# Output weights' squares taken a group ahead in quarters, and their split in halves, in a hybrid attention layer

## The chip, the cores and the metric

One Trainium2 chip, one of its cores. The metric is the device time of one execution in microseconds (us): the median of 3 runs is 599.39 (599.29 to 605.95). The engines are named as in the profile: PE (TensorE matmul), PEld (its weight load), DVE (VectorE), ACT (ScalarE), POOL (GpSimd), SP (SyncE, which issues most DMAs here).

## The reference

One encoder layer over 1024 tokens of width 1024, in float32. The input is normalised, one projection makes the columns of two head groups, both are gated, and a second projection `w_out` of 1024 x 1024 is added to the residual and normalised:

```python
h = _rmsnorm(x, norm_gain[l])
proj = h @ w_in[l]
q_a, k_a, v_a, g_a, q_b, k_b, v_b, g_b = jnp.split(proj, split_at, axis=-1)
...
o_a = _gqa_blocked(q_a, k_a, v_a) * jax.nn.silu(g_a)
o_b = _neighbourhood_attn(q_b, k_b, v_b, na_rpb[l])   # 8 heads, over a 16 x 64 grid
o_b = o_b * jax.nn.silu(g_b)
mixed = jnp.concatenate([o_a, o_b], axis=-1)
x = x + mixed @ w_out[l]
...
return _rmsnorm(x, final_norm_gain)
```

## The kernel before

**Numbers in two parts.** Matmuls run in float16. Each float32 operand is scaled and split into a high part and a residual (low part), and a product is three matmuls: high x high, high x low, low x high. So a group of weights has to be prepared before PE can use it.

**Groups of weights.** The weights come in 17 groups of 256 columns: 0 to 12 of `w_in`, 13 to 16 of `w_out`. A group is `raw[g]`, 128 partitions x 8 x 256 in float32 (1 MB). Its preparation has five steps. `load_w` issues its load on POOL's queue; `raw` has two buffers, so group g + 2 is loaded when group g is split. `prep_a` squares it on ACT and adds up each partition (`wss`). `prep_b` sums over the partitions by a one-column matmul on PE into the PSUM tile that the next projection will use, and DVE and POOL make the scale of it. `prep_c` writes the high part as two copies on ACT (`whl`), and `prep_d` the residual as two instructions on DVE.

**Steps.** The program is laid out in steps of a class `Flow`. In the stage of this document (from about 355 us on) a step takes one head of one block of 128 tokens of the neighbourhood attention: 8 blocks x 8 heads. "Head 4_3" below is head 3 of block 4, and the order prints its maximum as `mx4_3`. A step computes the head's scores on PE (`b_qk`, L674 and L675), the biased scores and their maximum on DVE (L682, L684), and two exponentials on ACT (L685, L686); in the next step the residual of the exponentials on DVE and its transposing DMA on SP (`b_lo`, L691, L693); and five steps on, the product with the values on PE (`b_pv`, L704 to L706). Between scores and products each step fills PE with about three chunks of 6 projection matmuls (`fill`; L368 in the profile): the gates of groups 9 to 12, then the output projection `out_gen`, which takes blocks 0 to 3 through group 13, then 14, 15 and 16, and block 4 behind them. DVE adds its result to the residual rows `x2b` (L773), which are loaded on POOL's queue (L764). `at(delay, position, ...)` puts a piece of work so many steps later.

**What sets the order.** PE's instructions stay as they are written. Behind the opening block, those of ACT, DVE, POOL and SP are put in order by a scheduler when the program is built, by its own idea of what will be ready; each engine then runs its list in order. So a piece can stand several steps ahead of where `at` put it.

**Where the preparation starts.** `prep(g + 1)` is called when the first chunk of group g starts. It puts `prep_a` one or two steps later (`PREP`), and `pend`, one step on, lets `sums_now` call `prep_b` in the middle of the next projection; `prep_c` and `prep_d` follow a step later, then the load of g + 2.

Of the kernel before, what the change touches and what calls it, by code (L numbers as in the profile page):

```python
# [10 lines left out]
BF16 = mybir.dt.bfloat16  # L11
# [5 lines left out]
P = 128  # L17
KC = 8
# [14 lines left out]
LN_P = 14.0 * float(np.log(2.0))  # L33
# [10 lines left out]
class Flow:  # L44
# [8 lines left out]
    def at(self, delay, pos, fn, *a):  # L53
        self.due.setdefault((self.slot + delay, pos), []).append((fn, a))
# [35 lines left out]
def kernel(ctx: ExitStack, tc: tile.TileContext, x: bass.AP, w: bass.AP, wo: bass.AP,  # L90
# [57 lines left out]
    def tn(name, n=1, tag="t"):  # L148
        return tiny.tile([P, n], F32, tag=tag, name=name)
# [47 lines left out]
    def col(i, n=1):  # L197
        return sm[:, i:i + n]
# [68 lines left out]

    wss = {}

    def prep_a(g):  # L270
        if g < 15:
            t = whl.tile([P, 2, KC, GC], F16, tag="whl", name=f"whl{g}")
        else:
            if g == 15:
                late["w"] = one.tile([P, 2, 2, KC, GC], F16, tag="hT0", name="whl15")
            t = late["w"][:, g - 15]
        wp[g] = (t[:, 0], t[:, 1])
        wss[g] = tn(f"wss{g}", 1, "ws")
        if g:
            act.activation(wp[g][0].bitcast(BF16), raw[g], AF.Square, accum_out=wss[g])  # L280
            return
        late["half"] = tn("wssh", 1, "ws")
        act.activation(wp[g][0][:, :4].bitcast(BF16), raw[g][:, :4], AF.Square, accum_out=late["half"])

    def prep_a2(g):
        dve.tensor_tensor_reduce(out=wp[g][0][:, 4:].bitcast(BF16), in0=raw[g][:, 4:], in1=raw[g][:, 4:], scale=1.0,
                                 scalar=late["half"], op0=OP.mult, op1=OP.add, accum_out=wss[g])

    def prep_b(g):
        pt = ahead.append(proj_tile(f"wt{g}")) or ahead[-1]  # L290
        top = [a.bitcast(BF16)[:, 1:2] for a in (mh[:, :1], wss[g])]
        pe.matmul(pt[:, 0, :1], top[0].to_broadcast([P, P]), top[1], start=True, stop=True)
        dve.tensor_scalar(wss[g], pt[:, 0, :1], -2.0 ** -27, 1e-30, op0=OP.mult, op1=OP.add)  # L293
        pool.tensor_tensor(col(S_ + g), wss[g], mh[:, :1], op=OP.pow)  # L294

    def prep_c(g):
        for i in range(0, KC, KC // 2):
            s = slice(i, i + KC // 2)
            act.activation(wp[g][0][:, s], raw[g][:, s], AF.Copy, scale=col(S_ + g))  # L299

    def prep_d(g):
        ready.add(g)
        n = KC if g == 0 else KC // 2
        for i in range(0, KC, n):
            s = slice(i, i + n)
            dve.scalar_tensor_tensor(wp[g][1][:, s], raw[g][:, s], col(S_ + g), wp[g][0][:, s], op0=OP.mult, op1=OP.subtract)  # L306
# [8 lines left out]
    ready = set()  # L315

    def prep_e(g):
        dve.reciprocal(col(RC + g), col(S_ + g))
# [725 lines left out]
```

## Time and profile before

| | |
|---|---|
| median of the runs | 599.39 us |
| the profiled execution | 600.28 us, span 598.5 us |
| mean granted PE clock | 0.974 |
| busy, share of the span | PE 89%, DVE 74%, ACT 65%, POOL 20% |
| whole squares of groups 13 to 16 on ACT start at | 457.06, 474.88, 481.91, 502.17 us |
| their first copies on ACT start at | 471.64, 489.26, 507.89, 525.18 us |
| their loads are issued by POOL at | 397.40, 426.95, 475.58, 496.08 us |

A row of a timeline gives start, duration, engine, line, operation, what is written and read, the size and the count; in brackets stands how long the engine sat idle ahead of it, and what released it. `wt` and `po` are PSUM tiles of projections, `whl` the two parts of weights, `mhl` those of the mixed rows. The times of a count of several run from the first start to the last end.

### The profile page before, as it was taken

Reading aid. Unit: us, or ns where it says so; the run is one execution under the profiler, and the core shown is the slowest. Engines: PE = TensorE matmul, PEld = TensorE weight load, DVE = VectorE, ACT = ScalarE, POOL = GpSimd, SP = SyncE. Lnnn points to the kernel's source line nnn. Section 1 sums busy time; section 2 is a strip of 40 time slices with the busy share of each in tenths; the row PEclk is TensorE's granted clock in tenths of the full one; section 3 lists DMA queues with packets and bytes.
Section 4 is the critical chain, followed back from the end, with each engine's and each line's share of the span. In section 5 each row is a group of like instructions: output and inputs, shape, how many; then the busy total and the mean of one; then the engine's idle time right before and its main releaser. Section 6 shows DMA issues by size and latency. Waiting matters only on the chain.

```text
span 598.5 us, 13870 instructions
## 1 busy us (share of the span) xinstructions
PE 530.8 (89%) x5541; PEld 404.4 (68%) x5541; DVE 440.9 (74%) x986; ACT 391.0 (65%) x647; POOL 121.8 (20%) x150
## 2 busy tenths in 40 slices
PE   2587989979979989998989979999999789889894
PEld 1366878758856545556768857887877567668684
DVE  4689676987978968975988947585878767778332
ACT  5553445777768858875868826677779986774210
POOL 2395788510100000000100000010111221122100
PEclk9979989989999989999899999999999899999898
DMA  8989533799999999999899983467576996699422
GB/s 233 225 162 243 112 108 68 143 187 215 195 192 188 206 209 181 221 191 208 179 188 213 230 214 79 90 133 96 128 116 123 180 200 146 138 146 190 92 61 70
DMA packets 245972, 97.26 MB, mean 162 GB/s; under 512 B 236562, under 2 KB 237202, under 8 KB 243987
## 3 DMA queue, kind: packets, MB, share of 16 engines
q1 hardware_dynamic: 242306, 75.66, 70.8%
q0 software_dynamic: 3312, 19.92, 11.7%
q8 instruction: 43, 0.70, 0.5%
q10 hardware_dynamic: 288, 0.79, 0.5%
q14 instruction: 23, 0.18, 0.1%
HBM read 31.33 MB, written 4.19 MB: 59 GB/s over the span
## 4 chain that ended last, share of the span: by engine, by line
PE 48%; DMA 18%; DVE 14%; issue 8%; ACT 5%; POOL 4%; SPq 1%; DVEq 0%; POOLq 0%; ACTq 0%
PE pj L368 15%; DMA ar<-ar 10%; PE wt L368 8%; PE kb L368 5%; PE po L368 4%; PE s L591 3%; PE s L593 3%; PE pv L622 2%; PE pv L624 2%; PE pv L623 2%; DVE whl L306 2%; DMA ar<-mhl 2%; POOL nt L416 1%; PE sb L675 1%; DMA x2b<-in_x_dram 1%
## 5 line engine op out<-in xcount | busy, mean ns | idle before, releaser
L368 PEld LDWEIGHTS <-hT 128*128 128x128 f16 x2112 | 205.8, 100 | 68.9 <-DMA hT<-xhl 14.7
L368 PE MATMUL pj<-whl,hT 128*128 128x256 f16 x1584 | 187.6, 274 | 3.9 <-DMA hT<-xhl 2.5
L602 ACT ACTIVATE ar<-s,nm,sm 128x1024 f32<-128x1024 f32 x64 | 76.9, 1202 | 43.6 <-DVE nm L600 35.8
L600 DVE CUSTOM_DVE_ANT_0 ar<-s,sm 128x1024 bf16<-128x1024 f32 x64 | 81.9, 1279 | 18.9 <-PE s L593 18.6
L368 PE MATMUL wt<-whl,hT 128*128 128x256 f16 x528 | 70.9, 294 | 13.8 <-ACT whl L299 7.1
L608 DVE TENSOR_TENSOR ar<-ar 128x1024 f16<-128x1024 f32 x64 | 77.9, 1218 | 5.4 <-ACT ar L603 5.4
L603 ACT ACTIVATE ar<-ar 128x1024 f16<-128x1024 f32 x64 | 67.5, 1056 | 6.5 <-DVE ar L608 5.3
L368 PE MATMUL po<-whl,mA 128*128 128x256 f16 x384 | 65.8, 277 | 0.0
L685 ACT ACTIVATE rq<-ar,mx,sm 128x384 f32<-128x384 f32 (+1 forms) x64 | 43.0, 672 | 30.8 <-DVE mx L684 30.6
L294 POOL TENSOR_TENSOR sm<-wss,mh 128x1 f32<-128x1 f32 x17 | 12.7, 749 | 240.4 <-DVE wss L293 160.6
L368 PEld LDWEIGHTS <-mA 128*128 128x128 f16 x512 | 48.8, 100 | 12.5 <-issue 5.3
L368 PE MATMUL po<-whl,ar 128*128 128x256 f16 x192 | 53.1, 277 | 0.0
L622 PE MATMUL pv<-va,ar 128*128 128x64 f16 x384 | 39.9, 195 | 12.0 <-DMA ar<-ar 12.0
L306 DVE SCALAR_TENSOR_TENSOR whl<-raw,sm,whl 128x1024 f16<-128x1024 f32 (+1 forms) x33 | 44.7, 1371 | 2.3 <-ACT whl L299 2.3
L622 PEld LDWEIGHTS <-ar 128*128 128x128 f16 x384 | 35.1, 99 | 16.6 <-DMA ar<-ar 14.3
L686 ACT ACTIVATE ar<-ar,mx,sm 128x384 f16<-128x384 f32 (+1 forms) x64 | 42.8, 673 | 1.0
L299 ACT ACTIVATE whl<-raw,sm 128x1024 f16<-128x1024 f32 x34 | 37.0, 1136 | 5.9 <-POOL sm L294 5.8
L624 PE MATMUL pv<-va,ar 128*128 128x64 f16 x384 | 39.9, 195 | 0.0
L623 PE MATMUL pv<-va,ar 128*128 128x64 f16 x384 | 39.8, 195 | 0.0
L591 PE MATMUL s<-kTa,rq 128*128 128x512 f16 x128 | 39.4, 391 | 0.3 <-ACT ar L602 0.3
L682 DVE CUSTOM_DVE_ANT_0 ar<-sb,bias 128x384 f32<-128x384 f32 x48 | 26.6, 554 | 17.2 <-PE sb L675 14.3
L691 DVE TENSOR_TENSOR ar<-rq,ar 128x384 f16<-128x384 f32 (+1 forms) x64 | 34.1, 533 | 4.4 <-ACT ar L686 4.4
(183 smaller groups left out, 1012.2 us busy)
## 6 DMA issues: line engine op xcount, KB each, us to landing
raw<-in_w_dram POOLq DMA_DIRECT2D x11, 1024.0 KB, 6.3
raw<-in_wo_dram POOLq DMA_DIRECT2D x4, 1024.0 KB, 6.1
ar<-in_x_dram SPq DMA_DIRECT2D x7, 512.0 KB, 6.4
khh<-ar SPq DMA_DIRECT2D x16, 128.0 KB, 4.1
x2b<-in_x_dram POOLq DMA_DIRECT2D x4, 512.0 KB, 6.4
x<-in_x_dram POOLq DMA_DIRECT2D x4, 512.0 KB, 6.3
out_dram<-x2b SPq DMA_DIRECT2D x8, 256.0 KB, 3.3
ar<-ar SPq DMA_TRANSPOSE x112, 4.5
```

Source lines behind the costliest of these rows:

```text
L306: dve.scalar_tensor_tensor(wp[g][1][:, s], raw[g][:, s], col(S_ + g), wp[g][0][:, s], op0=OP.mult, op1=OP.subtract)
L368: pe.matmul(*o[0], **o[1])
L591: pe.matmul(s[:, c * 512:(c + 1) * 512], q, kTa[:, 4 * c:4 * c + 4, hh], start=True, stop=False)
L600: dve.tensor_tensor_reduce(out=hl[:, 1].bitcast(BF16), in0=s, in1=col(SHA).to_broadcast([P, 1024]), scale=col(NSA), scalar=3e38, op0=OP.ad ...
L602: act.activation(p32, s, AF.Exp, bias=nm, scale=col(SCA), accum_out=sums[hh, u][:, h:h + 1])
L603: at(0, "post", lambda: act.activation(hl[:, 0], p32, AF.Copy))
L608: dve.tensor_tensor(hl[:, 1], p32, hl[:, 0], op=OP.subtract)
L622: pe.matmul(o, pt[:, kt], va[:, kt, hh, 0], start=kt == 0, stop=False)
L623: pe.matmul(o, pt[:, kt], va[:, kt, hh, 1], start=False, stop=False)
L624: pe.matmul(o, pt[:, 8 + kt], va[:, kt, hh, 0], start=False, stop=kt == 7)
L685: act.activation(p32, t, AF.Exp, bias=mx, scale=col(SCB + hh), accum_out=sums["b", u][:, h:h + 1])
L686: act.activation(hl[:, 0], t, AF.Exp, bias=mx, scale=col(SCB + hh))
```

## The change

For groups 13 to 16 the squares are taken in quarters (`prep_q`, four ACT instructions of 128x512 with one `wss` column each, whose unused output goes to a free place in `rq`) and one group earlier: those of 13 in steps 7 to 10 behind the start of group 11, those of g + 1 in steps 2 and 3 behind the start of group g - 1's projection. `prep_b` then adds four one-column matmuls instead of one. `prep_c` and `prep_d` run in halves, in steps 1 and 2 after `prep(g)`, and the load of g + 2 follows in step 3. Groups 0 to 12 stay as they were, but for the order around them.

```diff
+SQ13 = (7, 8, 9, 10)
...
-PREP = {2: 4, 3: 0, 4: 2, 12: 0, 13: 0}
+PREP = {2: 4, 3: 0, 4: 2, 12: 0}
...
-    def prep_a(g):
+    def alloc_wp(g):
...
         wp[g] = (t[:, 0], t[:, 1])
-        wss[g] = tn(f"wss{g}", 1, "ws")
+
+    def prep_a(g):
+        alloc_wp(g)
+        wss[g] = [tn(f"wss{g}", 1, "ws")]
...
+    def prep_q(g, i):
+
+        junk = carve(rq, 17408, [512], BF16).rearrange("p (k c) -> p k c", c=GC)
+        if i == 0:
+            wss[g] = [tn(f"wss{g}_{k}", 1, "ws") for k in range(4)]
+        act.activation(junk, raw[g][:, 2 * i:2 * i + 2], AF.Square, accum_out=wss[g][i])
...
     def prep_b(g):
         pt = ahead.append(proj_tile(f"wt{g}")) or ahead[-1]
-        top = [a.bitcast(BF16)[:, 1:2] for a in (mh[:, :1], wss[g])]
-        pe.matmul(pt[:, 0, :1], top[0].to_broadcast([P, P]), top[1], start=True, stop=True)
-        dve.tensor_scalar(wss[g], pt[:, 0, :1], -2.0 ** -27, 1e-30, op0=OP.mult, op1=OP.add)
-        pool.tensor_tensor(col(S_ + g), wss[g], mh[:, :1], op=OP.pow)
-
-    def prep_c(g):
-        for i in range(0, KC, KC // 2):
-            s = slice(i, i + KC // 2)
+        top = [a.bitcast(BF16)[:, 1:2] for a in (mh[:, :1], *wss[g])]
+        n = len(wss[g])
+        for i in range(n):
+            pe.matmul(pt[:, 0, :1], top[0].to_broadcast([P, P]), top[1 + i], start=i == 0, stop=i == n - 1)
+        t = wss[g][0]
+        dve.tensor_scalar(t, pt[:, 0, :1], -2.0 ** -27, 1e-30, op0=OP.mult, op1=OP.add)
+        pool.tensor_tensor(col(S_ + g), t, mh[:, :1], op=OP.pow)
+        scaled.add(g)
+
+    HALVES = [slice(i, i + KC // 2) for i in range(0, KC, KC // 2)]
+
+    def prep_c(g, halves=HALVES):
+        assert g in scaled
+        for s in halves:
             act.activation(wp[g][0][:, s], raw[g][:, s], AF.Copy, scale=col(S_ + g))
 
-    def prep_d(g):
+    def prep_d(g, halves=HALVES):
+        for s in halves if g else [slice(0, KC)]:
+            dve.scalar_tensor_tensor(wp[g][1][:, s], raw[g][:, s], col(S_ + g), wp[g][0][:, s], op0=OP.mult, op1=OP.subtract)
+        if halves[-1] != HALVES[-1]:
+            return
         ready.add(g)
...
+    def squares(g, slots):
+        for i, k in enumerate(slots):
+            at(k, "pre", prep_q, g, i)
+        at(slots[-1], "mid", pend.append, g)
+
     def prep(g):
-        d = PREP.get(g, 1)
-        at(d + 1, "pre", prep_a, g)
-        at(d + 2, "mid", pend.append, g)
+        if g < 13:
+            d = PREP.get(g, 1)
+            at(d + 1, "pre", prep_a, g)
+            at(d + 2, "mid", pend.append, g)
+            if g == 12:
+                squares(13, SQ13)
+            return
+        at(1, "pre", alloc_wp, g)
+        for i, h in enumerate(HALVES):
+            at(1 + i, "pre", prep_c, g, [h])
+            at(1 + i, "post", prep_d, g, [h])
+        if g + 2 < 17:
+            at(3, "pre", load_w, g + 2)
+        if g < 16:
+            squares(g + 1, (2, 2, 3, 3))
 
     def sums_now():
...
             prep_b(g)
+            if g > 12:
+                continue
             at(1, "pre", prep_c, g)
             at(1, "post", prep_d, g)
```

Line numbers grow by 36 from `prep` on: the scores are L710 and L711 after the change, maxima L718 and L720, exponentials L721 and L722, transposes L729, products L740 to L742, the projection L404, sums L809; quarters are L294, copies L316, residuals L320.

What the build's scheduler made of it, at three places. First ACT around head 4_3, where group 13's squares stood. Before:

```order
L686 ACTIVATE ar_78<-ar_78,mx4_2_5961,sm_97 128x384
L561 ACTIVATE ar_78<-pj11_3_5929,sm_97 128x512
L280 ACTIVATE whl13_6089,wss13_6090<-raw13_5183 128x2048
L685 ACTIVATE rq_79,sumb4_5856<-ar_78,mx4_3_6001,sm_97 128x384
L685 ACTIVATE rq_79,sumb4_5856<-ar_78,mx4_4_6050,sm_97 128x384
```

and of the change:

```order
L721 ACTIVATE rq_79,sumb4_5871<-ar_78,mx4_2_5975,sm_97 128x384
L597 ACTIVATE ar_78<-wt13_5853,sm_97 128x512
L316 ACTIVATE whl13_6103<-raw13_5183,sm_97 128x1024 x2
L721 ACTIVATE rq_79,sumb4_5871<-ar_78,mx4_3_6015,sm_97 128x384
L722 ACTIVATE ar_78<-ar_78,mx4_2_5975,sm_97 128x384
L722 ACTIVATE ar_78<-ar_78,mx4_3_6015,sm_97 128x384
L768 ACTIVATE mhl3_6119,os3_6118<-mA1_1063 128x512
```

The squares (L280, `wss13`) have become the copies (L316) at the same place, and the second exponentials of heads 4_2 and 4_3 stand behind them. Both halves stand together.

Second, ACT from head 4_6 to 5_1, ahead of the start of group 13's projection on PE. Before:

```order
L685 ACTIVATE rq_79,sumb4_5856<-ar_78,mx4_7_6179,sm_97 128x384
L686 ACTIVATE ar_78<-ar_78,mx4_7_6179,sm_97 128x384
L732 ACTIVATE mhl4_6443,os4_6442<-mA2_1064 128x512
L685 ACTIVATE rq_79,sumb5_6218<-ar_78,mx5_0_6219,sm_97 128x384
L732 ACTIVATE mhl5_7136,os5_7135<-mA2_1064 128x512
L299 ACTIVATE whl13_6089<-raw13_5183,sm_97 128x1024 x2
L686 ACTIVATE ar_78<-ar_78,mx5_0_6219,sm_97 128x384
L561 ACTIVATE ar_78<-pj12_3_6188,sm_97 128x512
L280 ACTIVATE whl14_6348,wss14_6349<-raw14_5581 128x2048
L685 ACTIVATE rq_79,sumb5_6218<-ar_78,mx5_1_6261,sm_97 128x384
```

and of the change:

```order
L721 ACTIVATE rq_79,sumb4_5871<-ar_78,mx4_6_6161,sm_97 128x384
L768 ACTIVATE mhl4_6479,os4_6478<-mA2_1064 128x512
L294 ACTIVATE rq_79,wss15_0_6375<-raw15_6199 128x512
L722 ACTIVATE ar_78<-ar_78,mx4_6_6161,sm_97 128x384
L721 ACTIVATE rq_79,sumb4_5871<-ar_78,mx4_7_6206,sm_97 128x384
L294 ACTIVATE rq_79,wss15_1_6376<-raw15_6199 128x512
L722 ACTIVATE ar_78<-ar_78,mx4_7_6206,sm_97 128x384
L721 ACTIVATE rq_79,sumb5_6245<-ar_78,mx5_0_6246,sm_97 128x384
L294 ACTIVATE rq_79,wss15_2_6377<-raw15_6199 128x512
L768 ACTIVATE mhl5_7172,os5_7171<-mA2_1064 128x512
L722 ACTIVATE ar_78<-ar_78,mx5_0_6246,sm_97 128x384
L721 ACTIVATE rq_79,sumb5_6245<-ar_78,mx5_1_6289,sm_97 128x384
```

Quarters of group 15's squares (`wss15`) now stand among the exponentials of heads 4_6 to 5_1, where group 13's copies and group 14's squares stood; the first is ahead of head 4_7's exponential.

Third, POOL's queue around the loads of groups 15 and 16. Before:

```order
L735 TENSOR_TENSOR os3_6105<-os3_6105,mh_83 128x1
L294 TENSOR_TENSOR sm_97<-wss13_6090,mh_83 128x1
L716 TENSOR_TENSOR ar_78<-ar_78 128x256
L764 DMA x2b_6318<-in_x_dram 128x1x1024 x2
L158 DMA raw15_6304<-in_wo_dram 128x2048
L760 COPY x2b_6318<-x2b_6318 128x1 x2
L764 DMA x2b_6318<-in_x_dram 128x1x1024 x2
```

and of the change:

```order
L159 DMA raw15_6199<-in_wo_dram 128x2048
L771 TENSOR_TENSOR os3_6118<-os3_6118,mh_83 128x1
L308 TENSOR_TENSOR sm_97<-wss14_0_6153,mh_83 128x1
L752 TENSOR_TENSOR ar_78<-ar_78 128x256
L800 DMA x2b_6343<-in_x_dram 128x1x1024 x2
L159 DMA raw16_6420<-in_wo_dram 128x2048
L796 COPY x2b_6343<-x2b_6343 128x1 x2
L800 DMA x2b_6343<-in_x_dram 128x1x1024 x2
```

Group 15's load (`raw15`) went from behind the first two loads of `x2b` to ahead of them, and group 16's from farther down the queue to ahead of the second two.

More of the change, by code (lines that the diff above doesn't have):

```diff
@@ L277, in prep_a @@
         wp[g] = (t[:, 0], t[:, 1])
-        wss[g] = tn(f"wss{g}", 1, "ws")
+    def prep_a(g):
+        alloc_wp(g)
+        wss[g] = [tn(f"wss{g}", 1, "ws")]
         if g:
-            act.activation(wp[g][0].bitcast(BF16), raw[g], AF.Square, accum_out=wss[g])
+            act.activation(wp[g][0].bitcast(BF16), raw[g], AF.Square, accum_out=wss[g][0])
             return
@@ L283, in prep_a @@
         act.activation(wp[g][0][:, :4].bitcast(BF16), raw[g][:, :4], AF.Square, accum_out=late["half"])
+    def prep_q(g, i):
[3 more added lines that the diff above has]
+        act.activation(junk, raw[g][:, 2 * i:2 * i + 2], AF.Square, accum_out=wss[g][i])
     def prep_a2(g):
         dve.tensor_tensor_reduce(out=wp[g][0][:, 4:].bitcast(BF16), in0=raw[g][:, 4:], in1=raw[g][:, 4:], scale=1.0,
-                                 scalar=late["half"], op0=OP.mult, op1=OP.add, accum_out=wss[g])
+                                 scalar=late["half"], op0=OP.mult, op1=OP.add, accum_out=wss[g][0])
@@ L302, in prep_d @@
+    def prep_c(g, halves=HALVES):
+        assert g in scaled
+        for s in halves:
+            act.activation(wp[g][0][:, s], raw[g][:, s], AF.Copy, scale=col(S_ + g))
+    def prep_d(g, halves=HALVES):
[3 more added lines that the diff above has]
+            return
         ready.add(g)
-        n = KC if g == 0 else KC // 2
@@ L304, in prep_d @@
-        for i in range(0, KC, n):
-            s = slice(i, i + n)
-            dve.scalar_tensor_tensor(wp[g][1][:, s], raw[g][:, s], col(S_ + g), wp[g][0][:, s], op0=OP.mult, op1=OP.subtract)
         if g > 1:
@@ L313, in prep_d @@
                 load_x2(2 * g - 26 + i)
-    ready = set()
+    ready, scaled = set(), set()
     def prep_e(g):
```

## The prediction

> **What bounds the kernel now.** I read the page first, then the waits of each engine by stage, then the timeline around every wait of TensorE.
>
> ```profile
> PE 530.8 (89%) x5541; PEld 404.4 (68%) x5541; DVE 440.9 (74%) x986; ACT 391.0 (65%) x647; POOL 121.8 (20%) x150
> PE 48%; DMA 18%; DVE 14%; issue 8%; ACT 5%; POOL 4%; SPq 1%; DVEq 0%; POOLq 0%; ACTq 0%
> ```
>
> PE is busy 89% of the span and holds half of the chain that ended last. So an edit on other engines pays only where PE stands idle. The table by stage of the last 175 us (columns: stretch, length, then busy time and instructions of PE, PEld, DVE, ACT and POOL, granted clock, DMA share, GB/s) shows where that is:
>
> ```profile
> 425.00:457.00 32.00, 32.00 (x341) 25.62 (x340) 25.20 (x74) 25.38 (x56) 4.29 (x7) 1.00 0.68 130
> 457.00:470.00 13.00, 11.93 (x122) 8.96 (x121) 11.41 (x38) 12.46 (x27) 2.68 (x4) 1.00 0.81 138
> 470.00:491.00 21.00, 17.82 (x171) 13.39 (x169) 13.36 (x48) 17.08 (x30) 5.87 (x11) 0.92 0.89 200
> 491.00:530.00 39.00, 31.84 (x327) 24.52 (x327) 29.77 (x95) 29.29 (x61) 5.61 (x9) 1.00 0.76 147
> ```
>
> Up to 457 us PE never stops. From 457 to 530 it loses 1.07 + 3.18 + 7.16 = 11.4 us. PE's waits between 457 and 530 us name what for, and the timeline of PE gives the places (in brackets the idle time ahead of the instruction):
>
> ```profile
> PE wt L368 <- DVE whl L306: 6.9, 5, 2.9
> PE wt L368 <- ACT whl L299: 2.4, 2, 2.1
> PE sb L704 <- DMA ar<-ar: 1.0, 1, 1.0
> PE sb L674 <- DVE mx L682: 0.7, 1, 0.7
> PE wt L292 <- DVE ar L569: 0.4, 1, 0.4
> ...
> 472.82 0.27 PE L368 MATMUL wt<-whl,mA 128*128 128x256 f16 x1 [2.13 <-ACT whl L299]
> 474.14 0.27 PE L368 MATMUL wt<-whl,mA 128*128 128x256 f16 x1 [1.05 <-DVE whl L306]
> 494.16 0.27 PE L368 MATMUL wt<-whl,mA 128*128 128x256 f16 x1 [2.91 <-DVE whl L306]
> 510.40 0.27 PE L368 MATMUL wt<-whl,mA 128*128 128x256 f16 x1 [1.05 <-DVE whl L306]
> 528.31 0.27 PE L368 MATMUL wt<-whl,mA 128*128 128x256 f16 x1 [1.68 <-DVE whl L306]
> ```
>
> So 9.3 of the 11.4 us are four waits, one at the start of each group of output weights (13 at 472, 14 at 494, 15 at 510, 16 at 528): PE has reached the group and its two parts aren't written. The first wait costs more than its length. The chain in order of time shows two equal pieces of work behind it, and two slices of the stage table show the clock:
>
> ```profile
> 475.54 3.74 PE wt L368 x18
> 479.97 2.07 PE wt L368 x18
> 482.73 0.78 PE wt L368 x6
> ...
> 476.00:477.00 1.00, 1.00 (x7) 0.69 (x6) 1.00 (x4) 1.00 (x3) 0.14 (x1) 0.50 1.06 242
> 480.00:481.00 1.00, 1.00 (x10) 0.89 (x10) 1.00 (x4) 0.00 (x0) 0.00 (x0) 1.00 0.91 336
> ```
>
> Eighteen matmuls take 3.74 us instead of 2.07, at a granted clock of 0.50: 1.67 us more. One undisturbed step (482.73 - 479.97) is 2.76 us.
>
> **The change part by part.** Sums are made against the profiled execution: 600.28 us with a span of 598.5. It lies 0.89 above the median of 599.39, which is taken off at the end.
>
> *The four waits.* The order of the change puts each group's copies and residuals (ACT's high part, DVE's low part) 4 to 6 heads earlier than before: group 13's copies stand where its squares stood (before head 4_3's exponential, instead of after 5_0's), group 14's behind 5_1's (before: 5_5's), group 15's behind 5_5's (before: 6_2's), group 16's behind 6_2's (before: 7_0's). At 2.76 us a step that is 11 to 17 us, more than the longest wait of 2.91. They need their scale earlier too; it comes from squares that are taken a group ahead. So I count all of them as gone: -9.3 us. For less, ACT or DVE would have to be 8 us late (11 - 2.9) at those rows.
>
> *The slow clock.* It follows the only wait with 3.2 us of idle PE in 4 us; the 2.91 us at 494 left the clock at 1.00 (fourth row of the stage table). I count it as going with the wait: -1.7 us. Were it there for another reason, the term would be 0. [...]
>
> *The squares in quarters.* ACT's rows of the whole square and of a 128x512 square with an accumulator (L797), which is a quarter's size, each with the start of the next; the pair of copies; and a residual on DVE:
>
> ```profile
> 457.06 1.90 ACT L280 ACTIVATE whl<-raw 128x2048 bf16<-128x2048 f32 x1
> 458.95 0.69 ACT L685 ACTIVATE rq<-ar,mx,sm 128x384 f32<-128x384 f32 x1
> ...
> 504.76 0.61 ACT L797 ACTIVATE ar<-x2b 128x512 bf16<-128x512 f32 x1
> 505.38 0.61 ACT L732 ACTIVATE mhl<-mA 128x512 bf16<-128x512 f32 x1
> ...
> 471.64 2.17 ACT L299 ACTIVATE whl<-raw,sm 128x1024 f16<-128x1024 f32 x2
> 473.72 0.69 ACT L686 ACTIVATE ar<-ar,mx,sm 128x384 f16<-128x384 f32 x1
> 492.83 1.28 DVE L306 SCALAR_TENSOR_TENSOR whl<-raw,sm,whl 128x1024 f16<-128x1024 f32 x1
> ```
>
> Start to start, the accumulator's read included, a whole square takes 1.89 us and four quarters 4 x 0.62 = 2.48: 0.59 more for each group, 2.4 for four. The pair of copies takes 2.08 either way. What matters is where they stand. Between 425 us and the start of group 14 at 491, ACT was busy 25.38 + 12.46 + 17.08 = 54.9 of 66 us. Now up to the same point of PE's work three whole squares (5.7) and two pairs of copies (4.2) leave, and ten quarters (6.2: groups 14 and 15, half of 16) and three pairs (6.2) come: 57.4. And the stretch is shorter by 3.2 + 1.7, so 61.1 us: ACT would be 94% busy. DVE gets group 14's two residuals (1.28 each at L306) in addition, and is at 50.0 + 2.6 of 61.1, 86%. The rows that bound what this costs PE: at 79% ACT (425 to 457) nothing was lost, at 96% (457 to 470) 1.07 of 13 us. So the term lies between 0, where the five steps from a head's scores to its use take up every delay, and 61.1 / 13 x 1.07 = 5.0. Any loss lowers ACT's share: on a line between the two rows it settles at about 3 us with ACT at 90%, and I take +3.0.
>
> *The sums on PE.* Each group adds three matmuls on a column and three weight loads, 12 in all. The row of the present one, and the matmul behind it:
>
> ```profile
> 467.07 0.18 PE L292 MATMUL wt<-wss,mh 128*128 128x1 bf16 x1 [0.40 <-DVE ar L569]
> 467.11 1.47 PE L368 MATMUL pj<-whl,hT 128*128 128x256 f16 x12
> ```
>
> Start to start it is 0.04 us, alone 0.18: 0.5 to 2.2 for 12, and I take +0.8, since others are pipelined behind them. Its wait for a PSUM tile (0.40) was in the lost time above.
>
> *The loads on POOL's queue.* Group 15's load moves ahead of the residual rows x2b of blocks 0 and 1, group 16's from 496 us to just ahead of x2b for blocks 2 and 3. The rows of today:
>
> ```profile
> 484.95 1.05 POOL L764 DMA_DIRECT2D x2b<-in_x_dram  x2 [0.17 <-POOL x2b L760]
> 492.43 0.48 DVE L773 SCALAR_TENSOR_TENSOR x2b<-po,rw,x2b 128x256 f32<-128x256 f32 x1 [1.13 <-DMA x2b<-in_x_dram]
> 496.08 0.63 POOL L158 DMA_DIRECT2D raw<-in_wo_dram  x1 [5.73 <-DVE mx L684]
> 502.17 1.91 ACT L280 ACTIVATE whl<-raw 128x2048 bf16<-128x2048 f32 x1 [1.69 <-DMA raw<-in_wo_dram]
> ```
>
> DVE already waited 1.13 us for x2b, 7.5 us after its issue. With another MB ahead of it, at the 200 GB/s of that stage, 2.1 MB take 10.5 us: x2b lands up to 3 us later against DVE's need. Behind the waiting sum stand group 15's residuals (not needed for 10 us) and the scaled maximum of head 5_7, so PE sees between 0 and 3 us of it: +1.0, low because a head has five steps to its use.
>
> *Sum:* 600.3 - 9.3 - 1.7 + 3.0 + 0.8 + 1.0 = 594.1; on the median's scale 593.2 us, 1.0% faster.
>
> **The rivals.** *Full gain.* ACT at 94% and the loads cost PE nothing: 600.3 - 11.0 + 0.5 = 589.8, 588.9 on the median's scale. For it: the quarters no longer hold an exponential back for 1.9 us, and 13 us at 96% lost only 1.07. Against it: ACT and DVE wait for each other in order.
>
> *The first half of the gain is lost.* ACT becomes the bound from 440 to 490: PE now stops for late transposes (as it did for 1.0 us at L704) instead of for weights. 5.0 and 1.7 for a clock that drops again, with 3 for x2b: 600.3 - 11.0 + 5.0 + 1.7 + 0.8 + 3.0 = 599.8, or 598.9: no change. For it: in the order of the change, ACT has the gate's tanh of group 12's third block ahead of head 4_5's exponential, and it waits for PE.
>
> *Slower: ACT stands before a load.* The first quarter of group 15's squares was put ahead of head 4_7's exponential, and those of 14 and 16 stand as far ahead. Their load goes out only after the previous group's second residual, and ACT is in order, so all exponentials behind wait.
>
> ```profile
> 461.53 0.55 DVE L682 CUSTOM_DVE_ANT_0 ar<-sb,bias 128x384 f32<-128x384 f32 x1
> 468.66 0.63 ACT L732 ACTIVATE mhl<-mA 128x512 bf16<-128x512 f32 x1 [0.47 <-DVE mA L570]
> ```
>
> Head 4_6's maximum began at 461.53; group 13's second residual now stands just ahead of it, so load 15 goes out at about 463 and lands 6.1 later (502.17 - 496.08), at 469. ACT got to that place at 468.66. So it waits about 0.5 us, and 3.5 if DVE is 3 us late; it decides from where the five steps (13.8 us) are used up. Three loads at 3.5 in place of the 3.0 above, and the clock down once: 600.3 - 11.0 + 10.5 + 1.7 + 0.8 + 1.0 = 603.3, or 602.4. Against it: the wait of 1.69 at 502 left PE running.
>
> That the scales don't come earlier after all is ruled out by the order; I give it no chance of its own.
>
> **How the numbers follow.** Forecast 593.2: 0.50, its own range 590 to 597. Full gain 588.9: 0.17. First half lost 598.9: 0.22. Slower 602.4: 0.11. The range of 8 in 10 reaches from just below the full gain to just above no change: 588.3 to 600.5. 2% is 12 us, about what a measurement of this kernel can tell from no change: faster needs 587.4 or less, more than all terms give unless the smaller waits (0.7, 1.0) go too: 0.04. Slower needs 611.4, beyond the slower rival: 0.02. Within 2%: 0.94.
>
> **What would show it right or wrong.** PE's waits for the two parts of the output weights should fall from 9.3 us to under 1; the clock should hold 1.00 from 470 to 490; PE should wait 2 to 5 us in places that had none: for transposes (L740 now), for maxima, or for PSUM tiles. The first quarters of groups 14 to 16 should show waits of ACT for the loads of 0 to 2 us. It is wrong if PE still waits for the parts, if ACT waits more than 3 us for a load and PE right after it, or if the sum of PE's new waits is over 6 us.

## The result: 0.6% slower, and the profile after

The changed kernel takes 605.44 us (median of 20 runs, 602.35 to 610.87), the kernel before, run beside it, 602.12 us (20 runs, 598.18 to 606.87). The ratio is 1.0063 with a 95% interval of 1.0038 to 1.0087: 3.8 us slower, where 1% faster was forecast. It lies above the range that was given.

The two profiled executions already differ where nothing was changed. The page of the changed kernel, and ACT's first copies of group 12 (a pair of two, L299 before, L316 after), from the timelines of before and of after:

```profile
span 604.0 us, 13919 instructions
PE 532.8 (88%) x5553; PEld 405.5 (67%) x5553; DVE 441.0 (73%) x986; ACT 392.6 (65%) x671; POOL 122.4 (20%) x150
...
421.96 2.19 ACT L299 ACTIVATE whl<-raw,sm 128x1024 f16<-128x1024 f32 x2 [0.29 <-POOL sm L294]
425.13 2.19 ACT L316 ACTIVATE whl<-raw,sm 128x1024 f16<-128x1024 f32 x2 [0.29 <-POOL sm L308]
```

Those copies come 3.2 us later, and not by the change: the products of the first head, 0_0, already start 3.16 us later (370.54 us before, 373.70 after), more than 40 us ahead of the change's first quarter of a square (416.07). Over the kernels below for which a tail is given, the place varies from 420.7 to 426.5 us, in no order. So I compare from there to the end of the span, called the tail from here on: 598.5 - 421.96 = 176.5 us before, 604.0 - 425.13 = 178.9 after. That is 2.3 us more, in one execution of each; verdicts go by the ratios.

PE's waits from 425 us to the end, of after, then the row of before for the heads' transposes, and the places of the larger ones of after in PE's timeline:

```profile
PE pvb L740 <- DMA ar<-ar: 8.0, 4, 4.6
PE sb L740 <- DMA ar<-ar: 4.4, 3, 2.0
PE sb L710 <- DVE mx L718: 1.3, 2, 1.0
PE sb L740 <- DVE mx L718: 1.2, 2, 0.8
PE wt L305 <- DVE ar L605: 0.4, 1, 0.4
...
PE sb L704 <- DMA ar<-ar: 3.6, 3, 1.7
...
472.85 0.23 PE L740 MATMUL pvb<-rq,ar 128*128 128x64 f16 x1 [4.56 <-DMA ar<-ar]
500.25 0.20 PE L740 MATMUL pvb<-rq,ar 128*128 128x64 f16 x1 [2.28 <-DMA ar<-ar]
504.78 0.32 PE L710 MATMUL sb<-khh,qTb 128*128 128x384 f16 x1 [1.01 <-DVE mx L718]
```

Not one wait for weights is left. In their place PE waits 12.4 us for the heads' transposes (3.6 before) and 2.5 for maxima (0.7 before): in all 14.9 us in waits over 0.3 us, where the kernel before has 13.5. The stages show the same, and the clock (columns as in the table of before):

```profile
457.00:470.00 13.00, 11.28 (x119) 8.77 (x116) 11.11 (x31) 10.46 (x22) 1.91 (x3) 1.00 0.65 144
470.00:491.00 21.00, 18.11 (x168) 13.47 (x169) 14.23 (x43) 16.53 (x38) 4.69 (x9) 0.84 0.86 172
491.00:530.00 39.00, 32.26 (x335) 24.62 (x333) 27.02 (x93) 27.80 (x62) 7.60 (x12) 1.00 1.01 179
...
470.00:480.00 10.00, 7.11 (x52) 4.71 (x53) 5.31 (x22) 7.91 (x21) 1.45 (x2) 0.66 0.90 179
471.00:472.00 1.00, 0.00 (x0) 0.00 (x0) 0.31 (x1) 0.98 (x5) 0.00 (x0) 0.79 1.15 189
```

The half clock stands behind the wait of 4.56 us as it stood behind the 2.13 of before. By the last two rows it begins at 471.6, inside the wait, and holds for 10 x 0.34 x 2 = 6.8 us (each microsecond from 472 to 478 has a granted clock of 0.50), 5.5 of them after the wait: 2.7 us lost, where 1.7 were. How that wait comes about is read from ACT's timeline, then DVE's, the chain, and POOL's load:

```profile
458.65 0.63 ACT L768 ACTIVATE mhl<-mA 128x512 bf16<-128x512 f32 x1 [2.42 <-DMA ar<-mhl]
459.28 0.69 ACT L721 ACTIVATE rq<-ar,mx,sm 128x384 f32<-128x384 f32 x1
460.54 2.17 ACT L316 ACTIVATE whl<-raw,sm 128x1024 f16<-128x1024 f32 x2
463.31 1.29 ACT L722 ACTIVATE ar<-ar,mx,sm 128x384 f16<-128x384 f32 x2
...
465.57 0.52 DVE L727 TENSOR_TENSOR ar<-rq,ar 128x384 f16<-128x384 f32 x1
...
466.15 6.65 DMA ar<-ar
...
465.85 0.62 POOL L159 DMA_DIRECT2D raw<-in_wo_dram  x1 [1.38 <-DVE sumb L747]
```

ACT first stands 2.42 us for a transpose of the mixed rows. Then head 4_2's first exponential (459.28) is followed by group 13's copies (460.54), which PE doesn't need before 480; the second exponential comes at 463.31, the residual at 465.57. Its transposes then run beside group 15's load, and take 6.65 us (2.81 in the kernel before).

### The profile page after: what moved, and what is told of

Its sections match the earlier page's. It is cut to its first block, busy times and chain, and to the rows that moved or that the text cites. A ratio compares the mean times of both kernels' runs of the same rounds, so it can differ in the third digit from the quotient of the medians.

```text
span 604.0 us, 13919 instructions
## 1 busy us (share of the span) xinstructions
PE 532.8 (88%) x5553; PEld 405.5 (67%) x5553; DVE 441.0 (73%) x986; ACT 392.6 (65%) x671; POOL 122.4 (20%) x150
## 4 chain that ended last, share of the span: by engine, by line
PE 50%; DMA 19%; DVE 12%; POOL 7%; issue 6%; ACT 3%; SPq 2%; DVEq 0%; POOLq 0%; ACTq 0%
PE pj L404 17%; DMA ar<-ar 13%; PE wt L404 7%; PE kb L404 5%; PE po L404 4%; PE s L627 3%; PE s L629 3%; POOL nt L452 2%; PE pv L658 2%; PE sb L711 2%; PE pv L660 2%; PE pv L659 2%; POOL ar L464 2%; DMA hT<-xhl 2%; POOL ar L460 1%
## 5 line engine op out<-in xcount | busy, mean ns | idle before, releaser
L404 PEld LDWEIGHTS <-hT 128*128 128x128 f16 x2112 | 207.1, 100 | 70.1 <-issue 15.6
L404 PE MATMUL pj<-whl,hT 128*128 128x256 f16 x1536 | 185.9, 277 | 4.1 <-DMA hT<-xhl 2.6
L404 PE MATMUL wt<-whl,hT 128*128 128x256 f16 x576 | 74.7, 287 | 14.4 <-ACT whl L316 7.4
L404 PE MATMUL po<-whl,mA 128*128 128x256 f16 x416 | 71.1, 277 | 0.0
L721 ACT ACTIVATE rq<-ar,mx,sm 128x384 f32<-128x384 f32 (+1 forms) x64 | 43.1, 673 | 30.9 <-DVE mx L720 23.7
L404 PE MATMUL po<-whl,ar 128*128 128x256 f16 x208 | 57.4, 276 | 0.0
L404 PEld LDWEIGHTS <-mA 128*128 128x128 f16 x512 | 48.3, 99 | 9.1 <-issue 2.4
L658 PE MATMUL pv<-va,ar 128*128 128x64 f16 x384 | 39.9, 195 | 12.8 <-DMA ar<-ar 12.8
L718 DVE CUSTOM_DVE_ANT_0 ar<-sb,bias 128x384 f32<-128x384 f32 x48 | 26.5, 552 | 26.8 <-PE sb L711 13.5
L320 DVE SCALAR_TENSOR_TENSOR whl<-raw,sm,whl 128x1024 f16<-128x1024 f32 (+1 forms) x33 | 45.0, 1376 | 0.2 <-ACT whl L316 0.2
L722 ACT ACTIVATE ar<-ar,mx,sm 128x384 f16<-128x384 f32 (+1 forms) x64 | 42.4, 672 | 0.8
L316 ACT ACTIVATE whl<-raw,sm 128x1024 f16<-128x1024 f32 x34 | 37.1, 1137 | 5.7 <-POOL sm L308 5.6
```

The source lines that it names most:

```text
L404: pe.matmul(*o[0], **o[1])
L658: pe.matmul(o, pt[:, kt], va[:, kt, hh, 0], start=kt == 0, stop=False)
L721: act.activation(p32, t, AF.Exp, bias=mx, scale=col(SCB + hh), accum_out=sums["b", u][:, h:h + 1])
L722: act.activation(hl[:, 0], t, AF.Exp, bias=mx, scale=col(SCB + hh))
```

## The experiments

Ratios are to the kernel before on the same chip, with 95% intervals; edits are shown against the changed kernel unless the kernel before is named. "Tail" is that of the profiled execution (before 176.5, after 178.9). Each edit also changes more than it says: from some point on the scheduler puts the work of ACT and DVE in another order.

**1. One part of the change alone.** In the first only group 13 is prepared by the change:

```diff
-        if g < 13:
+        if g != 13:
```

> Only group 13 is prepared by the change; 14 to 16 as before. Theory Q (place in the queues): group 13's copies and residuals, put among heads 4_2 and 4_3 on ACT and DVE, make 4_2's transposes late. It expects PE's wait of about 4.6 us for them and the half clock behind it to stand, and the weight waits of 14 to 16 to be back (2.9, 1.05 and 1.7): 1 to 3 us above the kernel before, ratio 1.002 to 1.005. Theory D (transfers): the loads of groups 15 and 16, moved to run beside the heads' transposes, make these slow. Load 15 goes out early here too, so D expects the 4.6 us as well, but load 16 is at its old place and the later waits for transposes (2.3, 1.0, 1.3, 2.0 us) are gone. If instead the sum of small costs along the whole stretch is to blame, the 4.6 us shrinks by more than half.

Measured: 1.0031 (1.0003 to 1.0059), tail 178.1. In the second group 13 is as before, the others as in the change (`if g < 14`, and group 13 calls `squares(14, (2, 2, 3, 3))`):

> Group 13 as before (square and copies just ahead of its use), 14 to 16 by the change. Theory Q expects no wait above 2 us for 4_2's transposes, PE's waits for group 13's parts back (2.1 and 1.05), and waits for transposes behind group 14's and 15's copies of 2 to 5 us in all: at the kernel before or up to 3 us below it (ratio 0.994 to 1.001). Theory D expects those waits to follow the loads: 15 and 16 go out where the change has them or a little later, so transposes issued within 3 us of a load still take 6 us or more, and the sum of PE's waits for transposes stays at 6 us or more (ratio 1.000 to 1.005).

Measured: 1.0041 (1.0002 to 1.0081), tail 179.5. In the first, the 4.6 us for 4_2 are gone, against both theories; other waits stand at other heads (3.03 us for a maximum at 487 us), and in the second one of 6.00 for a maximum at 489 us. Each part by itself costs about half to two thirds of the whole, by intervals that reach from almost nothing to all of it.

**2. The transfers.** The loads of groups 15 and 16 cut, then the x2b rows too, in the changed kernel and in the kernel before:

```diff
     def load_w(g):
+        if g > 14:
+            raw[g] = raw[g - 2]
+            pool.dma_start(raw[g][:, :1], wo[g - 13, :, :1])
+            return
...
         c = one.tile([P, 4, 1024], F32, tag="hT1", name="x2b")
+        pool.memset(c, 0.5)
...
-        pool.dma_start(x2[u], rows_of(x, u, 1024, 0, 1024))
+        n = 128 if u < 4 else 1024
+        pool.dma_start(x2[u][:, :n], rows_of(x, u, 1024, 0, n))
```

> The change, but the loads of groups 15 and 16 are cut to an eighth (128 kB each) and the rest of their weights stays that of groups 13 and 14: 7/8 of two loads of 1 MB are left out. Theory D expects the transposes that took 6.7 and 9.9 us to take 3 to 4, PE's wait for 4_2's transposes to shrink from 4.6 to under 2, the clock to hold, and the sum of PE's waits for transposes to fall from 12.4 to under 5: 5 us or more below the changed kernel, ratio to the kernel before 0.990 to 0.997. Theory Q expects the 4.6 to lose only what the transpose itself was too slow (about 3 us at most), if ACT and DVE stay as late; if nothing is owed to the loads, ratio 1.002 to 1.008 as with the change.

> The change with the bulk transfers of the last 170 us taken away: the loads of groups 15 and 16 and the x2b rows of blocks 0 to 3 are cut to an eighth each, 3.5 of 4 MB left out; weights and rows that are not loaded are old ones and a constant, written to x2b by one memset on POOL. Theory D (transfers): the heads' transposes share the DMA engines with these loads and become late; it expects transposes of 3 to 5 us, PE's waits after 425 us under 6 us in all (14.9 in the changed kernel), no half clock, ratio to the kernel before 0.983 to 0.993, and at least 5 us below the kernel before with the same transfers left out. Theory Q (place in the queues of ACT and DVE): the copies, residuals and quarters delay the exponentials whatever the loads do; it expects 10 us or more of waits and no gain over the kernel before with the same left out.

> The kernel before with the same transfers left out (7/8 of the loads of groups 15 and 16 and of the x2b rows of blocks 0 to 3). Both theories expect its four waits for output weights to stand (9 us, since the square comes just ahead of the use); D expects no more than 1 to 3 us of gain from the smaller loads, ratio 0.994 to 1.000, so that the change's gain shows as the difference to the change without them; Q expects the two kernels without loads to be within 2 us of each other.

Measured: small loads 1.0091 (1.0057 to 1.0125); all bulk cut, 0.9998 (0.9965 to 1.0031), tail 176.7; kernel before with it cut, 0.9914 (0.9881 to 0.9946), tail 170.1. With small loads 4_2's transposes take 2.79 us instead of 6.65 and its wait fell from 4.56 to 1.02 us; ACT's order is that of the changed kernel up to 466 us, so this part of the wait is the load's. But waits of 4.01 and 4.47 appeared at 486 and 511 us. Without the bulk the changed kernel still waits 9.7 us for transposes. And the kernel before gains as much from the missing transfers (0.9%) as the change does (0.7%), within the intervals: the transfers cost both, so they don't explain what the change lost by. D falls as the cause of the whole loss, though not as a cost.

**3. Parts or loads moved to a later place.** The copies held back by a head's maximum, and in the second only the two loads:

```diff
+    def hold(g):
+        pool.tensor_scalar(col(84), newest["mx"], 0.0, 1.0, op0=OP.mult, op1=OP.add)
+        pool.tensor_tensor(col(S_ + g), col(S_ + g), col(84), op=OP.mult)
...
+        if g > 14:
+            pool.tensor_copy(raw[g][:, 0, :1], newest["mx"])
         pool.dma_start(raw[g], w[g] if g < 13 else wo[g - 13])
```

> The change, with the two parts of each group held back until a later head's maximum is known (one column of the scale is multiplied by a one made from it on POOL): group 13's copies stand behind 4_6's first exponential in place of 4_2's, group 14's behind 5_3's in place of 5_1's, 15's behind 6_1's in place of 5_5's. Squares stay early and in quarters; the loads of 15 and 16, which follow the residuals, move by as much. Theory Q expects 4_2's transposes on time, no half clock, and the weight waits still at under 1.5 us in all: the sum of PE's waits falls by 6 us or more, ratio to the kernel before 0.985 to 0.997. Theory D expects the waits for transposes to move with the loads, to the heads about 4_6, and the sum to stay within 3 us of the change's: ratio 1.000 to 1.007.

> The change with the loads of groups 15 and 16 alone put back to about where the kernel before has them (each waits on POOL for the maximum of a later head, 5_0 and 5_6); squares, copies and residuals stay early as long as their data is there. D expects the 4.6 us wait for 4_2's transposes and the half clock behind it to go, as well as the wait of 2.3 us near 500 us, and weight waits of 0 to 3 us for groups 15 and 16: ratio to the kernel before 0.988 to 0.998. Q expects the 4.6 us to shrink to no less than 3, and ratio 1.002 to 1.008 as with the change.

Measured: 1.0114 (1.0071 to 1.0157) and 1.0343 (1.0293 to 1.0393). PE doesn't wait for 4_2's transposes in the first, and 0.85 us in the second, as Q and D had it; and yet both are far slower. PE's timeline of the second, with its waits for transposes, and POOL's:

```profile
489.86 0.23 PE L743 MATMUL sb<-ar 128*128 128x64 f16 x1 [12.59 <-DMA ar<-ar]
...
473.44 0.63 POOL L162 DMA_DIRECT2D raw<-in_wo_dram  x1 [0.30 <-POOL raw L161]
474.76 1.10 POOL L803 DMA_DIRECT2D x2b<-in_x_dram  x2
```

Group 15's load goes out 1.3 us ahead of x2b for blocks 0 and 1; 2 MB run beside the transposes of heads 4_5 to 4_7, those of 4_5 take 16.05 us, and PE stands for 12.59 us. In the kernel with later copies it is x2b and group 16's load about a microsecond apart, transposes of 19.23 us, and 10.63 us of waiting.

**4. ACT's work.** One quarter of each group's squares instead of four; the same in the kernel before; every quarter twice; the copies on POOL; one quarter and no bulk:

```diff
-            wss[g] = [tn(f"wss{g}_{k}", 1, "ws") for k in range(4)]
-        act.activation(junk, raw[g][:, 2 * i:2 * i + 2], AF.Square, accum_out=wss[g][i])
+            wss[g] = [tn(f"wss{g}_{k}", 1, "ws") for k in range(1)]
+            act.activation(junk, raw[g][:, 2 * i:2 * i + 2], AF.Square, accum_out=wss[g][i])
... the kernel before:
+            k = KC if g < 13 else 2
+            act.activation(wp[g][0][:, :k].bitcast(BF16), raw[g][:, :k], AF.Square, accum_out=wss[g])
... twice:
+        for _ in range(2):
... copies:
+            if g > 12:
+                pool.tensor_scalar(wp[g][0][:, s], raw[g][:, s], col(S_ + g), None, op0=OP.mult)
+                continue
```

> The change with one quarter of each group's squares instead of four: three quarters of the squares of groups 13 to 16 are left out, 12 small squares on ACT (12 x 0.62 = 7.4 us) and 12 matmuls on PE, so the scales differ. If ACT's time is what delays the heads (the prediction's term of ACT's share), PE's waits fall by 4 us or more and the ratio to the kernel before is 0.988 to 0.997. D expects only what the 12 matmuls and a little earlier exponentials give, 0 to 3 us below the changed kernel, ratio 1.000 to 1.006, with transposes of 6 us or more beside the loads as in the changed kernel.

> The kernel before, in its order, with a quarter of each output group's square instead of the whole (three quarters of the squares of groups 13 to 16 left out; 0.62 instead of 1.89 us on ACT, just ahead of the use). If less ACT time is all that helped the change with one quarter (which was 0.7% faster than the kernel before), this is at least as fast: four weight waits of 9.3 us shrink by up to 1.27 each, ratio 0.990 to 0.995. If the early place of the squares and parts brings something of its own once ACT has room, this one gains less: 0.995 to 1.000.

> The change with every quarter's square done twice: 16 more small squares on ACT, 16 x 0.62 = 9.9 us, nothing else. With one quarter instead of four, 7.4 us less on ACT made the kernel 7 us faster. If ACT's time at these places is the bound, this is 5 to 10 us slower than the changed kernel: ratio to the kernel before 1.014 to 1.023, in waits of PE for transposes and maxima. If ACT has room and the transfers set the waits, 0 to 3 us: ratio 1.006 to 1.011.

> The change with the high parts of groups 13 to 16 made on POOL instead of ACT (8 of 128x1024; ACT has 4 x 2.08 = 8.3 us less, nothing is left out). If ACT's time is the bound: PE's waits fall by 4 us or more, ratio 0.988 to 0.997, unless POOL's copies take over 3 us each and hold back the loads and the products behind them on its queue; then the waits move to x2b and the weights, ratio 1.00 to 1.02.

> The change with one quarter of the squares, and with the bulk transfers cut to an eighth as well (loads of groups 15 and 16, x2b rows of blocks 0 to 3). If ACT's time and the transfers each cost the heads something and the two add up, PE's waits after 425 us fall under 6 us, and it is 7 to 12 us below the kernel before: ratio 0.980 to 0.988, below the kernel before without these transfers (0.991). If they are one cost seen twice, it is no better than that: 0.990 to 0.995.

| kernel | ratio | interval | tail |
|---|---|---|---|
| change, one quarter | 0.9927 | 0.9893 to 0.9961 | 173.4 |
| before, one quarter | 0.9954 | 0.9927 to 0.9981 | 172.4 |
| change, each quarter twice | 1.0005 | 0.9977 to 1.0032 | 178.8 |
| change, copies on POOL | 0.9977 | 0.9943 to 1.0011 | 175.8 |
| change, one quarter, no bulk | 0.9853 | 0.9818 to 0.9887 | 164.8 |

Less work on ACT brings the change to the kernel before (copies) or below it (quarters). But 9.9 us more work did not slow it, against the theory of ACT's time: by the intervals, which don't overlap (up to 1.0032, from 1.0038), it is even faster than the change. The waits of the kernel with doubled quarters say why the sum hardly moves:

```profile
PE wt L306 <- ACT rq L295: 5.9, 1, 5.9
PE pvb L741 <- DMA ar<-ar: 4.7, 1, 4.7
PE sb L741 <- DMA ar<-ar: 2.2, 1, 2.2
```

PE stands once for 5.9 us before group 16's sum of squares, since the quarters are late, and half of the change's other waits are gone: 13.5 us in waits over 0.3 us, where the change has 14.9 and the kernel before 13.5. Waits are exchanged for one another. And with one quarter the kernel before is as fast as the change, within the intervals: with room on ACT, the early place brings nothing certain.

**5. The slots of the scores.** DVE's maxima wait for transposes in the change, by DVE's waits from 440 to 530 us, after first, then before:

```profile
DVE ar L718 <- DMA ar<-ar: 13.2, 6, 3.6
...
DVE ar L682 <- DMA ar<-ar: 2.8, 1, 2.8
```

There are five slots, so head 5_0's maximum can't be written before 4_3's transposes have landed. A sixth slot:

```diff
-        t, p32 = slot("t", [P, w], F32), slot("p32", [P, w], F32)
+        k6 = turn["t6"] = turn.get("t6", -1) + 1
+        t = six[:, :w] if k6 % 6 == 5 else area(k6 % 6 * 1536, [w], F32)
+        p32 = slot("p32", [P, w], F32)
```

> The change with six slots instead of five for a head's biased scores (the buffer that the maximum's instruction writes, the exponentials read and overwrite, and the transposes read); the room comes from a table that is dead by then and from smaller rings of three tiny tiles. Theory R (ring): with five slots, DVE can't start the maximum of a head before the transposes of the fifth head ahead of it have landed. Between 440 and 530 us DVE waited so for 13.2 us in the changed kernel and 2.8 in the kernel before, and behind it stand the residuals that feed the next transposes. R expects those waits under 4 us, PE's waits after 425 us 5 us or more below the 14.9 of the changed kernel, and a ratio to the kernel before of 0.985 to 0.998. Rival: PE's products wait for the same transposes anyway, so a slot more only moves the wait: DVE's waits fall, PE's stay at 12 us or more, ratio 1.002 to 1.008.

> The kernel before with the same six slots. R expects little, since its DVE waited only 2.8 us for transposes and the weight waits of 9.3 us stand: ratio 0.994 to 1.000. If a slot more helps both alike (by a better order of all the heads), it gains as much as the change does from it, 5 us or more: 0.985 to 0.992.

> The change with one quarter of the squares instead of four, and six slots. R with less work on ACT: PE's waits after 425 us under 7 us (10.5 with five slots), no weight waits, ratio to the kernel before 0.978 to 0.989, the best of all with its loads whole. If ring and ACT time are one cost, no better than with five slots: 0.989 to 0.996.

Measured: the change with six slots 1.0033 (1.0005 to 1.0061), the kernel before 0.9964 (0.9933 to 0.9994), the change with one quarter 0.9980 (0.9949 to 1.0012). DVE's waits for the transposes are gone entirely, and PE's are not:

```profile
PE pvb L743 <- DMA ar<-ar: 9.1, 2, 5.2
PE sb L743 <- DMA ar<-ar: 3.7, 3, 1.8
```

12.8 us of them, 12.4 with five slots. The rival was right: the slot isn't the bound. It is worth 0.4% to the kernel before, with an interval that just misses 1; to the change it brings 0.3% and to the change with one quarter it costs 0.5%, both with intervals that overlap those with five slots.

**6. The weight waits by themselves.** What was left was the first step of the sum. In the kernel before PE's products of groups 14 to 16 read group 13's parts, with no other edit:

```diff
-            hi, lo = wp[g]
+            hi, lo = wp[13]
```

> The kernel before, in which the products of groups 14 to 16 read group 13's two parts; the parts of 14 to 16 are made all the same, with the same squares, copies, residuals and loads at the same places, and read by nobody. So TensorE's three waits for them (2.9, 1.05, 1.68: 5.6 us) are gone and no work is moved earlier. Theory P (pace): the heads' chain of maximum, exponentials, residual and transposes sets the pace between 455 and 530 us; a pause of TensorE for weights only gives that chain time, and most of the 5.6 us comes back as waits for transposes and maxima: ratio 0.995 to 1.001. Rival (the step of the prediction): the waits are time lost to TensorE, and without them the kernel is 4.5 to 7 us faster: 0.988 to 0.993; then what the change loses is owed to the work that it moves.

> The same with a quarter of each output group's square instead of the whole (ACT has 3.8 us less before 510 us). Its weight waits for 14 to 16 were 3.9 us with the parts of their own. P expects 0 to 2 us of them as gain, ratio 0.992 to 0.996 (0.9954 with those waits); the rival expects all: 0.986 to 0.990.

Measured: 1.0013 (0.9986 to 1.0040), tail 175.7; with one quarter 0.9953 (0.9924 to 0.9981), where it was 0.9954 with the weight waits. Three waits (5.6 us in the first, 3.9 in the second) were taken away, and over the whole kernel nothing was gained, in neither. PE's waits of the first from 425 us on, and its largest two in the timeline:

```profile
PE sb L704 <- DMA ar<-ar: 7.3, 2, 4.2
PE wt L368 <- ACT whl L299: 1.6, 1, 1.6
PE sb L674 <- DVE mx L682: 1.5, 4, 0.6
PE wt L368 <- DVE whl L306: 1.1, 1, 1.1
PE pvb L704 <- DMA ar<-ar: 0.9, 1, 0.9
...
519.23 0.20 PE L704 MATMUL sb<-rq,ar 128*128 128x64 f16 x1 [4.23 <-DMA ar<-ar]
557.76 0.24 PE L704 MATMUL sb<-ar 128*128 128x64 f16 x1 [3.11 <-DMA ar<-ar]
...
519.00:523.00 4.00, 3.61 (x23) 2.11 (x24) 3.31 (x13) 2.37 (x5) 0.81 (x1) 0.58 0.57 120
```

What is left of the weight waits (2.7) is group 13's. The waits for transposes rose from 3.6 to 8.2 us, and behind the 4.23 at 519 the clock is halved once more (0.50 in each microsecond from 520 to 523).

This fits theory P, but it doesn't prove it, because the edit did move other work. In the traces the orders of DVE and ACT are those of the kernel before only up to 496 and 502 us. Up to there and somewhat beyond, the gain was there: PE starts the products of head 5_7 at 508.97 us where the kernel before starts them at 511.59, though its own first copies of group 12 come at 424.01 instead of 421.96, so it is 4.7 us ahead. It loses all of this at head 6_1, in the wait of 4.23 and the half clock behind it. ACT around it, in the kernel before and then in this one, and the chain of this one:

```profile
506.68 0.69 ACT L686 ACTIVATE ar<-ar,mx,sm 128x384 f16<-128x384 f32 x1
507.89 2.17 ACT L299 ACTIVATE whl<-raw,sm 128x1024 f16<-128x1024 f32 x2
...
507.57 2.17 ACT L299 ACTIVATE whl<-raw,sm 128x1024 f16<-128x1024 f32 x2
509.65 1.29 ACT L686 ACTIVATE ar<-ar,mx,sm 128x384 f16<-128x384 f32 x2
...
512.56 6.62 DMA ar<-ar
```

The new order has 6_1's second exponential behind group 15's copies instead of ahead of them, as the change has it at 4_2 with group 13's. Its transposes are issued at 512.56 instead of 508.03 and take 6.62 us instead of 2.73. In the kernel before PE waits 0.96 us for the transposes of the next head, 6_2 (at 521.01), so without the weight waits it might have waited longer there even in the old order; but no run shows that. What is shown is that three waits less were worth nothing in the kernels as the scheduler built them.

**7. A version better than both.** The kernel before with one quarter of the squares and six slots:

> The kernel before with a quarter of each output group's square and six slots for the scores: nothing left out that the result needs beyond the three quarters of the squares. Each alone gave 0.995 to 0.996. If they add up, 0.990 to 0.993; if both only shorten the same waits, 0.994 to 0.997.

Measured: 595.29 us, ratio 0.9895 (0.9858 to 0.9931), tail 169.7. Its scale comes from a quarter of the weights; the same scale is divided out behind the product. PE's waits from 425 us on:

```profile
PE wt L370 <- DVE whl L308: 4.4, 4, 1.3
PE sb L708 <- DMA ar<-ar: 2.3, 2, 1.7
PE wt L370 <- ACT whl L301: 1.8, 1, 1.8
```

It still waits 6.2 us for weights, and is 1.7% below the change, which waits for none (0.9895 / 1.0063 = 0.983).

## Why the prediction was wrong

**The four waits, -9.3 us.** As a statement on the trace it was right: the waits (seven in PE's rows, at four places) went, by the order as worked out. As a price it isn't confirmed. In part 6, 5.6 us of these waits are gone, and by the interval the time lies between 0.8 us less and 2.4 us more; in its trace the waits were a gain in full up to 517 us and were then lost at a head that stood late. No rival of mine asked whether such a gain lasts: each of them had it in full first and then charged something against it. In the change the parts that PE had waited for came sooner, and gaps as long opened elsewhere (9.3 us gone, 10.6 new).

**The slow clock, -1.7.** It came back behind the new wait of 4.56 us, and cost 2.7 us there: 1.0 more than before, not 1.7 less. The rival "first half of the gain is lost" had this, and the late transposes; it allowed 5.0 us for the waits, and 598.9 in all. The traces here show a granted clock of 0.50 at three places: behind the 2.13 and 1.05 us of group 13 in the kernel before (476 to 478 us), from inside the 4.56 us of the change on (472 to 478), and behind the 4.23 us of part 6 (520 to 523). Around the 2.91 us of the kernel before (491 to 500) and the 2.28 us of the change (499 to 504) it was 1.00. What decides between them isn't shown.

**ACT's share, +3.0: the step that failed.** This term was to hold what a fuller ACT would cost PE in the heads' waits. It was far too small, and argued from the wrong quantity. PE's waits for transposes grew by 12.4 - 3.6 = 8.8 us, those for maxima by 2.5 - 0.7 = 1.8: 10.6 in place of 3.0. ACT did not become full: between 425 and 491 us it was busy 27.72 + 10.46 + 16.53 = 54.7 of 66 us (forecast 94%, measured 83%). It waited in order, as ACT's waits from 455 to 530 us in the changed kernel show:

```profile
ACT rq L721 <- DVE mx L720: 7.6, 6, 3.2
ACT rq L721 <- DVE ar L727: 7.0, 5, 3.1
ACT mhl L768 <- DMA ar<-mhl: 3.8, 2, 2.4
ACT rq L294 <- DMA raw<-in_wo_dram: 0.4, 1, 0.4
```

A share of busy time doesn't show a chain whose engines wait for each other. I let the five steps from scores to use (13.8 us) take up most delays; head 4_2's delays on ACT and DVE and its slow transposes used them up together. With the load cut and the order the same, 1.02 us were left of 4.56; with the copies held back, 4_2's transposes take 2.82 us and land 3.4 us before PE needs them; with one quarter of the squares PE doesn't wait for 4_2, and 1.31 us for the next head. The steps had room for about one of the two delays.

**The sums on PE, +0.8.** In the one row that shows all four, they take 0.25 us where one took 0.18; nothing speaks against a size this small or smaller:

```profile
446.56 0.25 PE L305 MATMUL wt<-wss,mh 128*128 128x1 bf16 x4 [0.44 <-DVE ar L605]
```

**The loads, +1.0.** Wrong place. DVE's wait for x2b (1.13 us before) has no row in the waits of after; the load of group 15 hurt 4_2's transposes instead (2.79 us with an eighth of it, 6.65 with all), and those of 5_2 to 5_4, issued at 490 to 494 us beside group 16's load and x2b, took 9.6 to 10.9 us. ACT waited 0.4 us for the loads, within the 0 to 2 named, so the slower rival was wrong as well.

**The sum.** Waits: 9.3 us gone, 10.6 new; clock 1.0 worse: 2.3 us slower, as the tails differ; the ratio says 3.8. The sign of wrongness that the prediction named, new waits of PE over 6 us, is what came.

**What stays open.** The wait at 4_2, the largest, is accounted for by its two delays. That the change as a whole is 0.6% slower isn't pinned to one piece: its two parts each cost about half to two thirds of it, less ACT work takes it away, and twice the squares take it away too, so it may be that a new order of the heads' work on ACT and DVE by itself moves the time by as much. Part 6 has the same mixture. A kernel with the change's work in the order of before, or with the weight waits gone and the order held, would separate the order from the work; neither was tried.

## What to carry to other kernels

A wait of the busiest engine isn't a sure gain: here 9.3 us of waits went and 10.6 us of others came. Before moving work to fill such a gap, feed the waiting engine with something already there, as in part 6, and compare the order of the other engines with that of before: where a scheduler has changed it, the run tests both at once. Then price the move by the chain that it delays (here: maximum, exponentials, residual, transposes of one head, against the time until their use) and not by the busy share of its engines. What did help was less work on the chain's engines and one buffer more: 1% together.

## What was not expected of the hardware

Transposes took much of the DMA engines' time for few bytes: 74.4% of 17 us for 1.87 MB. In the kernel before with one quarter, two stretches of 17 us by queue, 440 to 457 with the transposes (of heads and of mixed rows) on the first queue, 495 to 512 with group 16's load on the other as well:

```profile
q1 hardware_dynamic: 7552, 1.87, 74.4%
...
q1 hardware_dynamic: 5317, 1.31, 40.2%
q0 software_dynamic: 144, 1.05, 21.3%
```

Over the time that their packets took, 1.87 MB in 0.744 x 17 us are 148 GB/s, and 192 in the second stretch; the plain load makes 1.05 MB in 0.213 x 17 us, 290 GB/s. So these transposes, of 2-byte data within SBUF, ran at half to two thirds of that load's rate; the prediction had reckoned with one mean over all transfers of a stage, 200 GB/s. In part 3, where 2 MB of loads were issued about a microsecond apart, transposes beside them took 16.05 and 19.23 us, and PE waited 12.59 and 10.63 us.
